# Gates computed first, the chunk inverse handed out in portions, and later stand-offs in a two-block layer kernel

## The chip, the cores and the metric

The kernel runs on one core of a Trainium2 chip. The metric is the device time of one execution in microseconds; lower is better. The time before is the median of three runs.

## The reference

The input is one sequence of 256 positions by 1024 channels in float32. Two layer blocks follow one another. The first has a short convolution branch and a gated delta rule branch, both from one wide projection `w_in`; their gated sum goes through `w_o`, and a convolution feed-forward follows. The second has dilated attention and retention, and a feed-forward. The change is mainly in the gated delta rule (8 heads, chunks of 64, key and value width 128):

```python
beta = jax.nn.sigmoid(b)
g = -jnp.exp(A_log) * jax.nn.softplus(a + dt_bias)
...
G = jnp.cumsum(g, axis=-1)
decay = jnp.exp(jnp.where(tril, G[..., :, None] - G[..., None, :], -jnp.inf))
L = jnp.where(strict, jnp.einsum('bnhid,bnhjd->bnhij', k_beta, k) * decay, 0.0)
rhs = jnp.concatenate([v_beta, k_beta * jnp.exp(G)[..., None]], axis=-1)
sol = lax.linalg.triangular_solve(eye + L, rhs, left_side=True, lower=True)
...
o = o * lax.rsqrt(jnp.mean(o * o, axis=-1, keepdims=True) + EPS) * norm_g
o = o * jax.nn.silu(z)
```

The projections a and b give the gates, q, k, v go through a causal convolution of four taps and a silu, and q and k are normalised by head. The kernel solves the triangular system by chunks of 128 with the inverse of (I + L).

## The kernel before

**Jobs and units.** Nearly all the time goes into dense products of 256 tokens with weights that are read once. A *job* is one block of weights of 1 MB (128 rows by 2048 values), and it has two halves, the *units*. SyncE (SP) loads a job into one of three raw buffers (`load_w`, line 316). For each unit ScalarE (ACT) copies 128x1024 values to a rounded high part H (`split_act`, line 143), and VectorE (DVE) subtracts it from the raw values to give the low part L (`tt`, line 146). TensorE (PE) then runs 24 matmuls of 128x256 in three passes of eight: Hh·H, Hl·H and Hh·L (`dense`, line 334). There are three buffers for H and L, and the split runs two units ahead of the matmuls.

**The order of the work.** Every engine works through its own queue in order. The program text makes that order: a main loop over the units advances *generators*. One kind evacuates a finished job (convolution taps, sigmoids, splits of the result), the other kind (`auxes`) carries the gated delta rule, the norms and the attention. Each `yield` hands control back, so the number of yields sets how many units later the next instructions stand in each queue. An instruction that waits holds everything behind it on its engine. The constants at the top of the file (`SUB_W`, `GAM_Y`, `AT_Y`, `SC_Y`, `SC_Z` and others) are such counts of yields; `D1_Q` and `SC_Q` choose which engine issues every second of some transfers.

**Order of the jobs.** K (4 jobs), ab (the gates, one small job of one unit), Q (4), the three parts of the short convolution interleaved (12), V (4), `w_a_out`, ga, z, gb, `w_b_out`, `w_o`, then the up and down jobs and the second block.

**The gated delta rule, by lines.** `gates` (from line 429) turns the projected a and b to tokens-by-heads with two small matmuls (line 432), takes sigmoid and exponentials on ACT, and evaluates a polynomial for the softplus by 28 small operations of 128x16 on GpSimd (POOL), ending in the tile `gg`. `gdn_decay` sums `gg` along the chunk with PE (lines 486 and 488), sends the sums through memory to all partitions (lines 498, 499) as `gam`, waits until the keys are done, and applies sixteen exponentials of 128x128, each with its own bias. `gdn_keys` transposes K (line 537) and sums squares on ACT. `gdn_main` forms K·Kᵀ (line 561), multiplies by `gam` on DVE and by beta on POOL into `U`, and scatters 32x32 blocks of U to memory with four transfers (line 573). They come back as `ebd`, 64 partitions of 32x32 (line 576).

**The substitution.** `subst` inverts the 64 blocks in place. `step(eng, i)` for i = 31 down to 1 is a multiply into `bt` and a subtraction from `ebd`, i·(32−i) values a partition, each depending on the one before. All 31 steps are issued to POOL at once. Then POOL clears Dm and Em, DVE copies the inverse transposed (line 596), two transfers write both forms to memory (line 598), and eight gathers bring the blocks to Dm and Em, 128x2048 each (line 604). `gdn_main` goes on when `sub_ok` is set: K·Qᵀ has been formed before (line 629), and now the first matmuls with Dm (line 649) and the doubling of the inverse follow (lines 651 to 672). Later the output o is normalised: rsqrt of q's norm and of o's norm, each twelve or so small operations on POOL, a multiply of o, and PE's transposes of o (line 772), which feed the `w_b_out` jobs.

**Elsewhere.** `up_evac` in the feed-forward multiplies gate and value on POOL (line 146) and splits the product, first high on ACT (`mh`), then low on DVE (`ml`). In the attention `qk_evac` scales q and k on ACT, and takes squares head by head (`jk`); an rsqrt on POOL (48 columns) follows, and PE transposes q and k (line 1167) `AT_Y` yields later.

## Time and profile before

| What | us |
|---|---|
| Median of three runs | 1133.23 (1131.77 to 1134.21) |
| Profiled execution | 1132.61 |
| Its span, first to last instruction | 1130.7 |
| PE busy | 1102.9 (98%) |
| DVE busy | 738.9 (65%) |
| ACT busy | 587.5 (52%) |
| POOL busy | 247.4 (22%) |
| Mean granted TensorE clock | 0.991 |

The span is what the trace covers, and the profiled execution has 1.9 us more around it. In the rows, a name like `L` or `ebd` is a tile of the program, with buffer numbers left out; line 146 is a helper that stands for all additions and multiplications, so tiles tell more than lines. An entry in brackets at a row's end is the time for which the engine stood idle before it, and the instruction that ended the wait.

### The profile page before, as it was taken

To read this page: it belongs to the slowest core of one execution; us is meant where nothing else is said; L and a number is where in the kernel's file an instruction comes from. 1 tells how busy PE (TensorE), PEld (TensorE's weight loads), DVE (VectorE), ACT (ScalarE), POOL (GpSimd) and SP (SyncE) were. 2 spreads that over 40 slices of the span, in tenths; PEclk is the share of its full clock that TensorE was granted. 3 is DMA by queue.
4 is the path that set the end of the run, shared out by engine and by line. 5 is a ranking of instruction groups with operands and counts; after the bars stand their busy time and mean duration, and the time that the engine had idled before them with its cause. 6 is when DMAs were issued, how large, how long until landed. Compare 5 with 4: busy or idle time off the path is not lost.

```text
span 1130.7 us, 20224 instructions
## 1 busy us (share of the span) xinstructions
PE 1102.9 (98%) x8340; PEld 1048.8 (93%) x8340; DVE 738.9 (65%) x985; ACT 587.5 (52%) x958; POOL 247.4 (22%) x290
## 2 busy tenths in 40 slices
PE   9989969999899999999999999999999999999998
PEld 8989969999899999999878799889999999898997
DVE  5767766345577888778854467557686657655554
ACT  7866425376445444444687544555474445444442
POOL 3575976021401222222201300001340001000000
PEclk9989989999999999999999999999999999999999
DMA  7566537343465466555565444453536555555652
GB/s 246 168 203 182 156 95 203 113 138 124 150 199 175 150 209 201 187 188 185 200 247 174 162 150 150 145 190 113 174 127 222 187 187 177 175 193 190 193 191 75
DMA packets 156080, 194.83 MB, mean 172 GB/s; under 512 B 6702, under 2 KB 133029, under 8 KB 155732
## 3 DMA queue, kind: packets, MB, share of 16 engines
q1 hardware_dynamic: 153888, 191.57, 52.1%
q0 software_dynamic: 848, 1.30, 0.5%
q8 instruction: 65, 1.06, 0.4%
q10 hardware_dynamic: 1252, 0.67, 0.2%
q14 instruction: 27, 0.22, 0.1%
HBM read 191.68 MB, written 1.84 MB: 171 GB/s over the span
## 4 chain that ended last, share of the span: by engine, by line
PE 75%; issue 8%; POOL 8%; DVE 5%; ACT 3%; DMA 1%; POOLq 0%; ACTq 0%; DVEq 0%
PE d L334 55%; PE x L334 13%; POOL bt L146 2%; POOL ebd L146 2%; DVE L L146 2%; ACT H L143 1%; DVE w L149 1%; POOL w L146 1%; DVE nl L149 1%; ACT w L143 1%; POOL nw L146 1%; PE x L1192 0%; ACT jk L143 0%; DVE X L146 0%; PE x L1167 0%
## 5 line engine op out<-in xcount | busy, mean ns | idle before, releaser
L146 DVE TENSOR_TENSOR L<-raw,H 128x1024 fp32r<-128x1024 f32 x354 | 443.5, 1259 | 252.0 <-ACT H L143 247.6
L143 ACT ACTIVATE H<-raw 128x1024 fp32r<-128x1024 f32 x355 | 369.7, 1053 | 192.6 <-PE d L334 134.0
L334 PE MATMUL d<-Hh,L 128*128 128x256 f32 x576 | 79.8, 282 | 9.3 <-DVE L L146 9.3
L334 PE MATMUL d<-nh,H 128*128 128x256 f32 x608 | 83.6, 279 | 2.2 <-ACT H L143 1.4
L334 PE MATMUL d<-Hh,H 128*128 128x256 f32 x576 | 84.6, 290 | 0.1
L334 PE MATMUL d<-nh,L 128*128 128x256 f32 x608 | 82.0, 277 | 0.0
L334 PE MATMUL d<-nl,H 128*128 128x256 f32 x608 | 81.9, 277 | 0.0
L334 PEld LDWEIGHTS d<-Hh,L 128*128 128x128 f32 x576 | 73.1, 192 | 9.5 <-DVE L L146 9.5
L334 PEld LDWEIGHTS d<-nh,H 128*128 128x128 f32 x608 | 76.7, 188 | 4.2 <-ACT H L143 1.6
L334 PE MATMUL d<-Hl,H 128*128 128x256 f32 x576 | 79.5, 281 | 0.0
L334 PEld LDWEIGHTS d<-Hh,H 128*128 128x128 f32 x576 | 74.3, 194 | 1.1 <-issue 0.4
L334 PEld LDWEIGHTS d<-nl,H 128*128 128x128 f32 x608 | 75.2, 188 | 0.0
L334 PEld LDWEIGHTS d<-nh,L 128*128 128x128 f32 x608 | 75.1, 188 | 0.0
L334 PEld LDWEIGHTS d<-Hl,H 128*128 128x128 f32 x576 | 73.1, 192 | 0.1
L334 PE MATMUL d<-H,x2h 128*128 128x512 f32 x208 | 57.3, 397 | 1.1 <-ACT H L143 1.1
L334 PE MATMUL d<-L,x2h 128*128 128x512 f32 x208 | 56.2, 392 | 0.0
L334 PE MATMUL d<-H,x2l 128*128 128x512 f32 x208 | 56.0, 391 | 0.0
L334 PE MATMUL d<-x2h,H 128*128 128x256 f32 x384 | 54.3, 284 | 0.0
L334 PE MATMUL d<-x2h,L 128*128 128x256 f32 x384 | 52.2, 278 | 0.0
L334 PE MATMUL d<-x2l,H 128*128 128x256 f32 x384 | 52.1, 278 | 0.0
L334 PEld LDWEIGHTS d<-x2h,H 128*128 128x128 f32 x384 | 48.7, 189 | 0.7
L146 POOL TENSOR_TENSOR gr<-w,w 128x512 f32<-128x512 f32 x8 | 11.8, 1472 | 171.4 <-ACT w L143 171.4
(394 smaller groups left out, 1939.7 us busy)
## 6 DMA issues: line engine op xcount, KB each, us to landing
raw<-in_w_in_dram SPq DMA_DIRECT2D x86, 1024.0 KB, 5.1
raw<-in_w_up_dram SPq DMA_DIRECT2D x38, 1024.0 KB, 5.3
raw<-in_w_down_dram SPq DMA_DIRECT2D x27, 1024.0 KB, 4.9
raw<-in_w_proj_b_dram SPq DMA_DIRECT2D x8, 1024.0 KB, 5.1
raw<-in_w_a_out_dram SPq DMA_DIRECT2D x4, 1024.0 KB, 6.4
raw<-in_w_b_out_dram SPq DMA_DIRECT2D x4, 1024.0 KB, 5.2
raw<-in_w_o_dram SPq DMA_DIRECT2D x4, 1024.0 KB, 5.2
raw<-in_w_out_dram SPq DMA_DIRECT2D x4, 1024.0 KB, 5.5
```

Of the source, the lines that this page charges most:

```text
L143: ACT.activation(out=out, in_=in_, func=func, **kw)
L146: eng.tensor_tensor(out=out, in0=a, in1=b, op=op)
L149: DVE.scalar_tensor_tensor(out=out, in0=in0, scalar=scalar, in1=in1, op0=op0, op1=op1)
L334: PE.matmul(out, lhsT=x if swap else w, rhs=w if swap else x, start=first and ps == 0, stop=last and ps == group[-1] and group is (order o ...
```

## The change

The ab job moves to the front of the list, and `id2`, which its transposes need, is made at the start. The polynomial of the gates moves from POOL to DVE, in four portions between yields. `gam` no longer waits for the keys; POOL subtracts the sums (four additions of 128x512), and two exponentials of 128x1024 take the place of the sixteen. The norm of k follows them. A yield in the key loop goes away, so that K·Kᵀ and what follows come earlier. All four scatters are issued by POOL. In the substitution the first eight steps go to DVE and the rest stays on POOL, with a yield after every four or two steps. The transposed copy moves to POOL, the clearing of Em, Dm and P stands between the transfers, and Em is gathered first. The rsqrt of q moves to DVE, right after Q·Kᵀ, with its square kept as `rq2`; the transposes of o come one unit later. V's sigmoid waits two yields longer, Q's one longer, K's as long as before (`SG_Y`). The first gate-times-value unit has a yield more, `AT_Y` is 5, one yield in the attention evacuation moves, and `late` splits a unit into two passes of two k-blocks each for two jobs.

```diff
-SUB_W = 11
+SUB_W = 1
-AT_Y = 4
+AT_Y = 5
-GAM_Y = 2
+GAM_Y = 4
-D1_Q = 0
+D1_Q = 2
+SG_Y = {8: 3, 0: 4, 16: 5}
-SC_Y = 3
-SC_Q = 1
-SC_Z = 3
+SC_Y = 2
+SC_Z = 4
...
             h3, l3 = w3(H, kh, n), w3(L, kh, n)
...
+            for ks in ((0, 1), (2, 3)) if late and half == 1 else (range(kh),):
...
-            yield
-            yield
-            yield
+            for _ in range(SG_Y[base]):
+                yield
             act(a2, acc, AF.Sigmoid)
...
-        tt(POOL, fl(s), fl(s), fl(u), MUL)
-        tt(POOL, fl(s2), fl(s), fl(s), MUL)
-        pts(fl(p), fl(s2), 1.0 / 17, MUL, 1.0 / 15, ADD)
+        tt(DVE, fl(s), fl(s), fl(u), MUL)
+        tt(DVE, fl(s2), fl(s), fl(s), MUL)
+        ts(fl(p), fl(s2), 1.0 / 17, MUL, 1.0 / 15, ADD)
+        yield
         for k in range(6, -1, -1):
-            tt(POOL, fl(p), fl(p), fl(s2), MUL)
-            pts(fl(p), fl(p), 1.0 / (2 * k + 1), ADD)
+            tt(DVE, fl(p), fl(p), fl(s2), MUL)
+            ts(fl(p), fl(p), 1.0 / (2 * k + 1), ADD)
+            if k in (2, 4):
+                yield
...
-        while "k_ok" not in gd:
-            yield
-        gdn_norm_k()
...
             tt(DVE, gam[:, sl, :], gam[:, sl, :], negm.unsqueeze(1).to_broadcast([128, 4, 128]), ADD)
-            if q % 2 == 0 and EXP1:
-                continue
-            yield
-            for u in range(8 * (q // 2) if EXP1 else 4 * q, 4 * q + 4):
-                act(gam[:, u, :], gam[:, u, :], AF.Exp, bias=ng[:, u:u + 1])
+            tt(POOL, gam[:, sl, :], gam[:, sl, :], ng[:, sl].unsqueeze(2).to_broadcast([128, 4, 128]), ADD)
+            if q % 2:
+                yield
+        for q in range(2):
+            yield
+            sl = slice(8 * q, 8 * q + 8)
+            act(gam[:, sl, :], gam[:, sl, :], AF.Exp)
         act(eg.rearrange("p a b -> p (a b)"), ng, AF.Exp, scale=-1.0)
+        while "k_ok" not in gd:
+            yield
+        gdn_norm_k()
...
             for i in range(31, 0, -1):
-                step(POOL, i)
+                step(POOL if i < 24 else DVE, i)
+                if i % (2 if 7 < i < 24 else 4) == 0:
+                    yield
...
-            POOL.memset(gd["Dm"], 0.0)
-            POOL.memset(gd["Em"], 0.0)
-            DVE.tensor_copy(out=blk, in_=eb.rearrange("p r c -> p c r"))
-            for dd, sb in ((d3, blk), (d2, eb)):
-                POOL.dma_start(out=dd.rearrange("b u r c -> (b u) r c"), in_=sb)
+            POOL.dma_start(out=d2.rearrange("b u r c -> (b u) r c"), in_=eb)
+            POOL.tensor_copy(out=blk, in_=eb.rearrange("p r c -> p c r"))
+            POOL.dma_start(out=d3.rearrange("b u r c -> (b u) r c"), in_=blk)
+            POOL.memset(gd["Em"], 0.0)
+            yield
             POOL.memset(gd["Dm"], 0.0)
...
-            for dd, dst in ((d3, gd["Dm"]), (d2, gd["Em"])):
+            for dd, dst in ((d2, gd["Em"]), (d3, gd["Dm"])):
...
+        yield
+        ts(sq, sq, EPS, ADD)
+        rsqrt(rq, sq, 16, dve=True)
+        rq2 = cst("rq2", [128, 16])
...
-        ts(sq, sq, EPS, ADD)
-        rsqrt(rq, sq, 16)
...
+    jobs.append(Job(load_w("w_in", 0, 8, 7168, 128), ab_mm, ab_evac, halves=1, start=(gates,), split=ab_split))
     for p in range(4):
         fm_job("w_in", 4096 + 256 * p, "x", qkv_evac(K, 8, p), start=(gdn_keys,) if p == 3 else ())
-    jobs.append(Job(load_w("w_in", 0, 8, 7168, 128), ab_mm, ab_evac, halves=1, start=(gates,), split=ab_split))
...
                 tt(POOL, md, ff.pop(("gs", m)), acc, MUL)
                 yield
+                if m == 0:
+                    yield
...
-            yield
             for i in range(2):
+                yield
                 for h in range(4):
```

Three places show how the queues change. The first is the polynomial of the gates (`spp`, `ss`; `KQ` is K's result, `w` a convolution's working tile). Before, on POOL:

```order
L146 TENSOR_TENSOR KQ_118<-w_541,w_542 128x256
L146 TENSOR_TENSOR w_674<-w_674,w_675 128x2x255
L146 TENSOR_TENSOR ss__657<-ss__657,su 128x16
L146 TENSOR_TENSOR ss_658<-ss__657 128x16
L168 TENSOR_SCALAR spp<-ss_658 128x16
L146 TENSOR_TENSOR spp<-spp,ss_658 128x16
L166 TENSOR_SCALAR spp<-spp 128x16
```

After, on DVE, `L` being a weight split:

```order
L146 TENSOR_TENSOR L_400<-raw_195,H_399 128x1024
L146 TENSOR_TENSOR ss__341<-ss__341,su 128x16
L146 TENSOR_TENSOR ss_342<-ss__341 128x16
L155 TENSOR_SCALAR spp<-ss_342 128x16
L146 TENSOR_TENSOR L_440<-raw_246,H_439 128x1024
L149 SCALAR_TENSOR_TENSOR w_433<-d_365,prm,w_433 128x254 x2
L149 SCALAR_TENSOR_TENSOR w_433<-d_365,prm,w_433 128x253 x2
L146 TENSOR_TENSOR spp<-spp,ss_342 128x16
L153 TENSOR_SCALAR spp<-spp 128x16
```

The polynomial has left POOL's queue and stands between DVE's splits, a portion at a time. The second place is the substitution's start and the copy on DVE. Before:

```order
L146 TENSOR_TENSOR w_2017<-d_1962,keep_1951 128x512
L146 TENSOR_TENSOR L_2020<-raw_1862,H_2019 128x1024
L146 TENSOR_TENSOR yal_1233<-w_2017,yah_1232 128x512
L596 COPY ebd_1391<-ebd_1391 64x1024
L146 TENSOR_TENSOR L_2058<-raw_1862,H_2057 128x1024
L146 TENSOR_TENSOR L_2094<-raw_1923,H_2093 128x1024
```

After:

```order
L146 TENSOR_TENSOR ebd_1290<-ebd_1290,bt_1490 64x28x4
L146 TENSOR_TENSOR L_1494<-raw_1210,H_1493 128x1024
L146 TENSOR_TENSOR AT_1475<-x_1476,gam_741 128x512
L146 TENSOR_TENSOR bt_1529<-ebd_1290 64x135
L146 TENSOR_TENSOR ebd_1290<-ebd_1290,bt_1529 64x27x5
L146 TENSOR_TENSOR bt_1532<-ebd_1290 64x156
```

Before, DVE had no step and had the copy of `ebd` ahead of a split; after, it has eight steps in two portions with a split between, and no copy. The third place is the end of the substitution on POOL (`scr` is memory). Before:

```order
L146 TENSOR_TENSOR bt_1674<-ebd_1391 64x31
L146 TENSOR_TENSOR ebd_1391<-ebd_1391,bt_1674 64x31
L594 MEMSET Dm_2051 128x2048
L595 MEMSET Em_2050 128x2048
L598 DMA scr_1386<-ebd_1391 64x1024
L598 DMA scr_1385<-ebd_1391 64x1024
L146 TENSOR_TENSOR w_2087<-w_2087,w_2088 128x2x255
L604 DMA Dm_2051<-scr_1386 32x16x32 x2
L604 DMA Em_2050<-scr_1385 32x16x32 x2
```

After:

```order
L146 TENSOR_TENSOR bt_1951<-ebd_1290 64x31
L146 TENSOR_TENSOR ebd_1290<-ebd_1290,bt_1951 64x31
L600 DMA scr_1284<-ebd_1290 64x1024
L601 COPY ebd_1290<-ebd_1290 64x1024
L602 DMA scr_1285<-ebd_1290 64x1024
L603 MEMSET Em_1992 128x2048
L605 MEMSET Dm_1993 128x2048
L608 MEMSET P_2062 128x2048
L614 DMA Em_1992<-scr_1284 32x16x32 x2
L614 DMA Dm_1993<-scr_1285 32x16x32 x2
L146 TENSOR_TENSOR w_2094<-w_2094,w_2095 128x2x255
```

The copy has come to POOL between the two transfers, a third memset has come ahead of the gathers, and the addition of V's convolution (`w`) now stands behind them. On PE the first matmuls with Dm stand behind the same unit as before, V's last.

## Rows read from the trace of the kernel before

**Rows 1.** Page, busy time by engine: busy us, share of the span, instructions.

```profile
PE 1102.9 (98%) x8340; PEld 1048.8 (93%) x8340; DVE 738.9 (65%) x985; ACT 587.5 (52%) x958; POOL 247.4 (22%) x290
```

**Rows 2.** What PE waited for: us in total, times, longest.

```profile
PE d L334 <- DVE L L146: 9.3, 1, 9.3
PE x L486 <- POOL gg L146: 3.5, 1, 3.5
PE x L772 <- POOL o L146: 3.4, 2, 3.2
PE x L1167 <- POOL k L146: 2.7, 2, 1.7
PE d L334 <- ACT H L143: 2.5, 2, 1.4
...
PE x L909 <- DVE sr L149: 0.3, 1, 0.3
```

**Rows 3.** Windows: us, busy of each engine, then PEclk (granted clock), DMA share, GB/s.

```profile
64.10:70.10 6.00, 6.00 (x27) 5.57 (x28) 0.21 (x1) 2.93 (x10) 5.26 (x7) 0.50 0.07 24
163.00:169.00 6.00, 2.37 (x11) 2.38 (x12) 6.00 (x7) 0.26 (x1) 2.81 (x3) 0.50 0.31 71
292.40:295.60 3.20, 3.20 (x15) 3.20 (x16) 1.58 (x2) 0.63 (x1) 3.20 (x6) 0.50 0.69 245
```

**Rows 4.** PE timeline (start, us, engine, line, operation, out<-in, [idle before]); long wait, Dm.

```profile
166.63 2.07 PE L334 MATMUL d<-Hh,L 128*128 128x256 f32 x8 [9.28 <-DVE L L146]
168.50 1.54 PE L334 MATMUL d<-Hh,H 128*128 128x256 f32 x8
169.88 1.07 PE L334 MATMUL d<-Hl,H 128*128 128x256 f32 x8
...
179.85 1.89 PE L649 MATMUL x<-Dm,U 128*128 128x64 f32 x16
```

**Rows 5.** Timeline of POOL: the last products of the gates.

```profile
63.84 0.36 POOL L146 TENSOR_TENSOR gg<-spp,nA 128x8 f32<-128x8 f32 x2
```

**Rows 6.** Timeline of DVE: a small operation and a weight split.

```profile
364.79 0.16 DVE L149 SCALAR_TENSOR_TENSOR sr<-nw,sr 128x2 f32<-128x2 f32 x1
364.87 1.23 DVE L146 TENSOR_TENSOR L<-raw,H 128x1024 fp32r<-128x1024 f32 x1
```

**Rows 7.** Timeline of ACT: a table load and what follows it.

```profile
26.97 1.28 ACT L143 ACT_TABLE_LOAD   x1
28.26 0.63 ACT L143 ACTIVATE w<-w 128x512 f32<-128x512 f32 x1
```

**Rows 8.** Timeline of POOL: U's last product and the scatters' issue (two, one by one).

```profile
101.22 1.04 POOL L146 TENSOR_TENSOR U<-U,bk 128x512 f32<-128x512 f32 x1 [1.76 <-DVE dec L568]
102.56 1.40 POOL L573 DMA_DIRECT2D scr<-U  x2 [0.30 <-POOL U L146]
```

**Rows 9.** DMA issues, 95 to 182 us: KB each, median us from issue to landing.

```profile
ebd<-scr POOLq DMA_DIRECT2D x1, 256.0 KB, 3.8
...
scr<-U POOLq DMA_DIRECT2D x2, 64.0 KB, 4.2
```

**Rows 10.** Timeline of POOL: the substitution and the first memset.

```profile
111.78 0.25 POOL L146 TENSOR_TENSOR bt<-ebd 64x31 f32<-64x31 f32 x1 [2.19 <-DMA ebd<-scr]
...
122.37 0.59 POOL L146 TENSOR_TENSOR bt<-ebd 64x207 f32<-64x207 f32 x1
...
123.70 0.59 POOL L146 TENSOR_TENSOR bt<-ebd 64x220 f32<-64x220 f32 x1
124.37 1.69 POOL L146 TENSOR_TENSOR ebd<-ebd,bt 64x220 f32<-64x220 f32 x1
...
161.12 1.81 POOL L594 MEMSET Dm<- 128x2048 f32 x1
```

**Rows 11.** Timeline of DVE: the copy.

```profile
161.17 4.27 DVE L596 COPY ebd<-ebd 64x1024 f32<-64x1024 f32 x1 [9.47 <-POOL ebd L146]
```

**Rows 12.** Line 604, the gathers of Dm and Em: issue to landing.

```profile
DMA to landing us min/median/max: 6.0/6.1/8.4
```

More of the change, by code (lines that the diff above doesn't have):

```diff
@@ L274, in startup @@
         param_cols(0, 128)
+        gd["id2"] = cst("id2", [32, 16])
+        tt(POOL, gd["id2"], ident[0:32, 0:16], ident[0:32, 16:32], ADD)
         for ft2 in range(4):
@@ L294, in startup_rest @@
         tt(POOL, gg, prm[:, 1, 96:104], prm[:, 1, 104:112], MUL)
-        gd["id2"] = cst("id2", [32, 16])
-        tt(POOL, gd["id2"], ident[0:32, 0:16], ident[0:32, 16:32], ADD)
         for ft2 in range(4):
@@ L335, in dense, with fm_job @@
                               stop=last and ps == group[-1] and group is (order or ORDER)[-1], skip_group_check=True)
-    def fm_job(name, c0, src, evac, k0=0, kt=8, n=256, ps_box=None, last=True, **kw):
+    def fm_job(name, c0, src, evac, k0=0, kt=8, n=256, ps_box=None, last=True, late=False, **kw):
         nf = n // 128
@@ L350, in mm @@
             xh, xl = S[src]
-            dense([(box[j // 2][:, j % 2, :], h3[:, k, 128 * j:128 * j + 128], l3[:, k, 128 * j:128 * j + 128],
-                    xh[:, half * kh + k, :], xl[:, half * kh + k, :], False,
-                    fresh and k == 0 and j % 2 == 0, last and half * kh + k == kt - 1 and j % 2 == 1)
-                   for k in range(kh) for j in range(nf)])
+            for ks in ((0, 1), (2, 3)) if late and half == 1 else (range(kh),):
+                dense([(box[j // 2][:, j % 2, :], h3[:, k, 128 * j:128 * j + 128], l3[:, k, 128 * j:128 * j + 128],
+                        xh[:, half * kh + k, :], xl[:, half * kh + k, :], False,
+                        fresh and k == 0 and j % 2 == 0, last and half * kh + k == kt - 1 and j % 2 == 1)
+                       for k in ks for j in range(nf)])
         jobs.append(Job(load_w(name, k0, kt, c0, n), mm, (lambda: evac(box)) if evac else None, **kw))
@@ L448, in gates @@
         fl = lambda t: t.rearrange("p a b -> p (a b)")
[L449 to L451 removed]
+        tt(DVE, fl(s), fl(s), fl(u), MUL)
+        tt(DVE, fl(s2), fl(s), fl(s), MUL)
+        ts(fl(p), fl(s2), 1.0 / 17, MUL, 1.0 / 15, ADD)
+        yield
         for k in range(6, -1, -1):
[L453 to L457 removed]
+            tt(DVE, fl(p), fl(p), fl(s2), MUL)
+            ts(fl(p), fl(p), 1.0 / (2 * k + 1), ADD)
+            if k in (2, 4):
+                yield
+        ts(fl(s), fl(s), -2.0, MUL)
+        tt(DVE, fl(p), fl(p), fl(s), MUL)
+        tt(DVE, fl(p), fl(p), fl(m), SUB)
         for c in range(2):
[L459 removed]
+            tt(DVE, g[:, c, :], p[:, c, :], nA[:, 0, :], MUL)
         yield
@@ L593, in subst @@
             gd["Em"], gd["Dm"] = alloc([16, 128], what="Em"), alloc([16, 128], what="Dm")
+            POOL.dma_start(out=d2.rearrange("b u r c -> (b u) r c"), in_=eb)
[3 more added lines that the diff above has]
+            yield
             POOL.memset(gd["Dm"], 0.0)
-            POOL.memset(gd["Em"], 0.0)
-            DVE.tensor_copy(out=blk, in_=eb.rearrange("p r c -> p c r"))
-            for dd, sb in ((d3, blk), (d2, eb)):
-                POOL.dma_start(out=dd.rearrange("b u r c -> (b u) r c"), in_=sb)
+            yield
+            gd["P"] = alloc([16, 128], what="P")
+            POOL.memset(gd["P"], 0.0)
             for _ in range(SC_Y):
                 yield
-            for dd, dst in ((d3, gd["Dm"]), (d2, gd["Em"])):
+            for dd, dst in ((d2, gd["Em"]), (d3, gd["Dm"])):
                 for b in range(4):
                     bs = slice(32 * b, 32 * b + 32)
-                    (POOL, (ACT, SP, POOL)[SC_Q])[b % 2].dma_start(out=dst[bs, :, bs], in_=dd[b].rearrange("u r c -> r u c"))
+                    (POOL, SP)[b % 2].dma_start(out=dst[bs, :, bs], in_=dd[b].rearrange("u r c -> r u c"))
             free(ebd)
@@ L633, in gdn_main @@
         free(gam, KQ[0])
+        yield
+        ts(sq, sq, EPS, ADD)
+        rsqrt(rq, sq, 16, dve=True)
+        rq2 = cst("rq2", [128, 16])
+        ts(rqs, rq, 128 ** -0.5, MUL)
+        tt(DVE, rq2, rqs, rqs, MUL)
         while "sub_ok" not in gd:
             yield
-        Em, Dm = gd["Em"], gd["Dm"]
-        P = alloc([16, 128], what="P")
-        POOL.memset(P, 0.0)
+        Em, Dm, P = gd["Em"], gd["Dm"], gd["P"]
         def half32(t, h):
@@ L746, in gdn_main @@
         fo = cst("fo", [128, 16])
-        ts(sq, sq, EPS, ADD)
-        rsqrt(rq, sq, 16)
-        POOL.tensor_scalar(out=rqs, in0=rq, scalar1=128 ** -0.5, scalar2=None, op0=MUL)
         yield
-        tt(POOL, sof, sof, rqs, MUL)
-        tt(POOL, sof, sof, rqs, MUL)
+        tt(POOL, sof, sof, rq2, MUL)
         POOL.tensor_scalar(out=sof, in0=sof, scalar1=1.0 / 128, scalar2=EPS, op0=MUL, op1=ADD)
@@ L1093, in _build @@
         for gate in (True, False):
-            fm_job("w_up", (0 if gate else 2816) + 256 * m, "xf", up_evac(m, gate), delay=(DG if gate else DV) if m == 0 else 0)
+            fm_job("w_up", (0 if gate else 2816) + 256 * m, "xf", up_evac(m, gate), delay=(DG if gate else DV) if m == 0 else 0,
+                   late=m == 0 and gate)
         if 0 < m < 9:
@@ L1117, in go @@
                 act(dst[:, i, :], box[i], AF.Copy, scale=S["r12"][:, i:i + 1])
-            yield
             for i in range(2):
+                yield
                 for h in range(4):
@@ L1551, in _build @@
     for m in range(16):
-        fm_job("w_up_2", 256 * m, "xn", up2_evac(m))
+        fm_job("w_up_2", 256 * m, "xn", up2_evac(m), late=m == 0)
         if m > 0:
```

4 lines of the change are left out of this document (removed).

## The prediction

> **What bounds the kernel now.** I read the page's busy times first: TensorE (PE) is busy 1102.9 us, 98% of the span [rows 1]. So the time is the matmuls plus the moments when PE stands still or runs slowly, and nothing else can be gained by this change, which leaves the number of matmuls as it is. The second view is what PE waited for [rows 2]: 9.3 us for a VectorE (DVE) weight split, 3.5 for the gates on GpSimd (POOL), 3.4 at the transposes of o, 2.7 at the attention transposes, 2.5 for a ScalarE (ACT) copy, 0.3 at a norm sum. With smaller ones it is under 25 us. The third view is the granted clock in windows behind these waits [rows 3]: 0.50 from 64.1 to 70.1, from 163 to 169 and from 292.4 to 295.6, that is 1.2 instead of 2.4 GHz, each right after a wait of over 3 us; work done there costs half its length again. That is 3.0 to 3.2 us after the gates, 1.6 after the transposes, and 1.45 after the long wait, where PE was only there from 166.6: its two first passes of eight matmuls took 2.07 and 1.54 instead of 1.07 [rows 4]. Shorter waits in the list were not followed by such a stretch.
>
> The profiled execution took 1132.6 us, 1.9 over its span and 0.6 under the median of the runs; I sum against it and add 0.6 at the end. Some 0.2%, 2.3 us, is what a measurement of this kernel can tell from no change.
>
> **The change, part by part**
>
> **Gates first.** Before, the polynomial stands on POOL behind K's convolution adds; its last product ends at 64.2 [rows 5], and PE waits. After, the ab job runs first, and 28 small operations stand on DVE in four portions between weight splits. A DVE operation of this size takes 0.16 us [rows 6]; with spacing I take 0.2, so 5.6 us of DVE work in four portions of about 1.4, which the lead of the splits over PE covers. Counted along DVE's queue gg is there at about 43.6 us, PE comes at about 45.3. Gone: 3.5 us of wait and 3.2 of half clock. Added: K's first unit now needs the second weight load, about 0.5 us later at the start, and two table loads stand on ACT ahead of the copy for the fifth unit. The load took 1.28 us and the next activation began 0.01 us after it ended [rows 7]; two of them, less what ACT was ahead, and the later DVE split: 1.0. Together −6.7 + 1.5 = **−5.2**; if the start costs nothing −6.7, if both loads come through whole −3.6.
>
> The Trainium skill, "ScalarE: Activation LUTs", section "What ACT_TABLE_LOAD costs", gives each switch about 1.28 us plus a drain of 1.38, 2.66 in all. By that the two loads would take 2.8 us more and this part would be −2.4; the trace shows no such drain between load and activation, so the row decides.
>
> **Decay.** Two wide exponentials replace sixteen; POOL gets four additions more, each about the length of the 1.04 us multiply of U [rows 8], plain work in a queue that has room there. But K's and Q's sigmoids on ACT now wait for adds behind them: 0 to 1 us for the copies of two units; I take **+0.5**.
>
> **Substitution, start.** K·Kᵀ stands three units (8.3 us) earlier on PE, and all before it is 5 us earlier; the chain through the norm of k on POOL, one unit later, eats part. Counted along POOL, U's last product is done at about 94.3 instead of 102.3. All four scatters are issued by POOL, two more than before at 0.7 [rows 8]; they land 4.2 us after issue, the load of the blocks 3.8 [rows 9]. So the first step, at 111.8 before [rows 10], comes at about 104.8. Eight steps go to DVE in two portions, 1.9 and 2.65 us, with a split between: done at about 111 (estimated as 0.16 us an instruction and the split's rate of 1.23 us for 1024 elements [rows 6]). By the two queues the splits behind them keep 2 to 4 us in hand; **+0.5** (0 to 2).
>
> **Substitution, rest.** 23 steps on POOL began at 122.4 and ended at 161.1 [rows 10]: 38.7 us. In it a subtraction took 1.69 us with a DVE split beside it, while the multiply of the same shape just before took 0.59; with the unheld length for every shape the 46 instructions come to 30.5, so holds make up 8.2 us. All fell in the 29.3 us before 151.7, since DVE then stood still waiting for POOL [rows 11]. In the changed kernel DVE goes on, so the last 9.4 us stretch at the same rate, 8.2 on 21.1: +3.6. End: 111 + 38.7 + 3.6 = 153.3.
>
> **The copy moves from DVE to POOL.** This ends the wait: DVE stood 9.47 us for the last step and copied for 4.27 [rows 11], with all splits behind it. Gone: 9.28 us and 1.45 of half clock, **−10.7**.
>
> **What is late next.** The inverse needs Dm at the same place of PE's queue as before, behind V's last unit. From the last step to Dm: the scatter's issue 0.6, the copy on POOL about 2.9 (1024 elements a row at the rate of the step of 220 elements in 0.59; at worst DVE's 4.27), a second issue 0.6, three memsets of 1.81 [rows 10], three gathers issued at 0.67, and 6.1 from issue to landing, at worst 8.4 [rows 12]. Sum 17.6, at worst 20.6. So Dm lands at about 170.9. PE got there at 179.85 [rows 4]; less 17.5 for the two waits and their slow clock, plus 2.5 for the costs above, it now arrives at 164.9. **A new wait of 6.0 us**, and half clock behind it, 1.45 to 3.2 by the other places, 2.0: **+8.0**. V's sigmoid on ACT stands behind a POOL add that comes after the gathers' issue, and falls into the same moment.
>
> **Transposes of o.** The rsqrt of q, on POOL just before them, moves to DVE long before, and the transposes go one unit later. 3.4 of wait and 1.6 of half clock go, the rsqrt of the output's norm still ends just when PE arrives: 0.3 stays. **−4.7.**
>
> **One yield in the first gate-times-value unit** puts ACT's copy of the product, which waits for a POOL multiply, behind the next weight copy: of the 2.5 us in the list [rows 2] the 1.4 here go, **−1.2**. The other 1.1, behind eight squarings, stays; the moved yield in the attention evacuation only swaps neighbours. **Splitting a unit in two passes** (late) cures 0.4 in the second block; in the first the norm sum ends last anyway [rows 2]. **−0.4.** **Attention transposes two units later**: 2.7 go, **−2.5**.
>
> Sum: −5.2 + 0.5 + 0.5 − 10.7 + 8.0 − 4.7 − 1.2 − 0.4 − 2.5 = −15.7, so 1116.9, and 1117.5 on the scale of the median.
>
> **The rivals**
>
> *No new wait.* Without any hold the 23 steps would take about 30.5 us (38.7 less 8.2). If they end by 147.3, Dm is in time: 8.0 less, **1109.5**. For it: where DVE stood still, from 151.7 on, the steps ran without a hold; against it: DVE is given its splits, and eight steps, at just that time. 0.2.
>
> *The wait at its worst.* Slow copy, slow landing, end at 154: Dm at 174.6, a wait of 9.7 with 3.2 of clock, **1122.4**. 0.16.
>
> *The scatters are late.* POOL's issues are held by DVE work as its adds are: the hold is 1.1 us [rows 10], four make 4.4; and if these four land as slowly as the slowest gather (8.4 for 4.2 [rows 9, 12]) it is 8.6 later in all. The first step then holds DVE until 113, PE waits for splits, and all up to Dm is 8.6 late: **1126.1**. Against it: both issues in the trace took 0.7 with DVE at work beside them [rows 8]. 0.07.
>
> The Trainium skill, "SBUF — State Buffer", section "A bandwidth-pool intuition that's wrong (but worth ruling out)", has this as a trap for transfers issued by GpSimd: about 620 ns alone, about 3100 beside a VectorE copy. By that four issues would be 9.6 us late, and the time 1127.1; the trace bears out the first figure and shows no case of the second.
>
> *Slower: POOL held nearly always.* Place: the 46 instructions of the 23 steps. A hold costs 1.1 [rows 10]; before, 7 or 8 fell on the first 28. Each further one moves the end, Dm and PE by its length. From 17 more (27 of 46, the end at 171.3) the change is slower by over 2.3 us; at 20 more it is 22 us, **1139.5**. Against it: it takes over twice the share of held instructions that the trace shows. 0.04.
>
> *The gates don't lead on DVE.* If the portions queue behind late splits, PE waits at the decay matmuls as before, up to 6.7: **1124.2**. 0.05.
>
> **How the numbers follow.** My forecast has 0.48, and its 1117.5 is the predicted time. The old waits go in every case and the new one's size is what is open, so the first three cases are faster whole. Late scatters and late gates (0.12 together) are faster singly; where both go wrong, and draw splits and sigmoids with them, the gain is used up: of their 0.12 I give 0.04 to the same and 0.02 to slower. With the 0.04 of the held POOL that is 0.90, 0.04, 0.06. The range holds the forecast, no new wait with a start that costs nothing (1109.5 − 1.5 = 1108) and the late scatters (1126), with 1 us more below for the terms taken at +0.5.
>
> **What would show it.** Right: no wait at the decay matmuls; no DVE wait of 9 us; a new PE wait of 4 to 9 us at the first Dm matmul with a 0.50 window behind it; no wait at the transposes of o over 0.5; 1.1 us left for ACT's copy. Wrong, if the Dm wait is missing or over 12, if splits wait behind the DVE steps near 107 us, or if a wait at the start exceeds 2 us.

## The result, and the profile after

The changed kernel takes **1151.8 us** (1151.0 to 1152.4, four runs) where the kernel before takes 1132.5 in the same session (1130.9 to 1134.2): a ratio of 1.016 (1.014 to 1.018), 19 us slower. The forecast was 1117.5 with a range of 1107 to 1126, so it is wrong in sign and 34 us off. The profiled execution took 1151.0, its span is 1149.2.

The page's busy times of the changed kernel, in us, with the share of the span and the number of instructions:

```profile
PE 1127.2 (98%) x8340; PEld 1073.6 (93%) x8340; DVE 750.5 (65%) x1033; ACT 586.0 (51%) x944; POOL 241.7 (21%) x245
```

Beside [rows 1] one thing stands out: PE executes the same 8340 matmuls and is busy 24.3 us longer. What it stood idle has become less. Its list of waits (line, what it waited for, us in total, times, the longest):

```profile
PE x L663 <- DMA Dm<-scr: 7.9, 1, 7.9
PE d L334 <- DVE L L146: 6.2, 6, 2.4
PE d L334 <- ACT H L143: 1.7, 2, 1.0
PE d L271 <- DVE warm L210: 1.4, 1, 1.4
PE x L920 <- DVE sr L149: 0.7, 1, 0.7
```

Against [rows 2] the waits for the gates, for the long weight split, at the transposes of o and at the attention transposes are gone; the new wait for Dm is there; and the weight splits are late six times by a little. The sum falls from 24 to 18 us. A reader who stops at the waits would call the change a success.

Two windows show where the 18.5 us of span come from: from the start to the first matmul with Dm (L663), and from there to the end. The columns are the stretch, its length, then the busy time and number of instructions of PE, the weight loads, DVE, ACT and POOL, and last the granted clock, the share of the DMA engines and GB/s. First the kernel before:

```profile
0.00:179.80 179.80, 165.43 (x1352) 162.62 (x1353) 126.09 (x173) 109.98 (x227) 118.36 (x163) 0.96 0.59 181
179.80:1130.00 950.20, 937.43 (x6990) 886.15 (x6989) 612.86 (x813) 477.55 (x731) 129.04 (x128) 1.00 0.52 171
```

The same of the changed kernel:

```profile
0.00:187.40 187.40, 170.99 (x1353) 165.53 (x1353) 137.90 (x224) 107.89 (x217) 115.35 (x132) 0.97 0.58 178
187.40:1149.00 961.60, 956.22 (x6988) 908.10 (x6988) 612.65 (x810) 478.15 (x729) 126.33 (x113) 0.99 0.51 168
```

Dm is reached 7.6 us later, after the same matmuls. Behind it PE is idle for 5.4 instead of 12.8 us, as forecast, yet busy 18.8 us longer with the same matmuls at nearly the same granted clock; the other 5.6 of the 24.3 us lie ahead of Dm. So there are two losses: matmuls that are slower each, and an early part that arrives later instead of earlier.

The slower matmuls can be seen in PE's timeline, in the middle of an undisturbed stretch (start, length, engine, line, out<-in, shapes, matmuls in the row). Before:

```profile
405.28 1.07 PE L334 MATMUL d<-nh,L 128*128 128x256 f32 x8
406.18 1.07 PE L334 MATMUL d<-nh,H 128*128 128x256 f32 x8
407.09 1.07 PE L334 MATMUL d<-nl,H 128*128 128x256 f32 x8
```

And the changed kernel in the same kind of unit:

```profile
420.78 1.12 PE L334 MATMUL d<-nh,H 128*128 128x256 f32 x8
421.74 1.12 PE L334 MATMUL d<-nl,H 128*128 128x256 f32 x8
422.70 1.12 PE L334 MATMUL d<-nh,L 128*128 128x256 f32 x8
```

Eight matmuls follow one another at 0.905 us before and at 0.96 us after, 113 and 120 ns for one. Nothing waits. Over the whole program, most passes of eight keep 113 or 118 ns a matmul before (about 370 and 410 passes), and 120 after (about 680).

### The profile page after: what moved, and what is told of

Same layout as the page of the kernel before. It is cut to its first block, busy times and chain, and to the rows that moved or that the text cites. A ratio compares the mean times of both kernels' runs of the same rounds, so it can differ in the third digit from the quotient of the medians.

```text
span 1149.2 us, 20224 instructions
## 1 busy us (share of the span) xinstructions
PE 1127.2 (98%) x8340; PEld 1073.6 (93%) x8340; DVE 750.5 (65%) x1033; ACT 586.0 (51%) x944; POOL 241.7 (21%) x245
## 4 chain that ended last, share of the span: by engine, by line
PE 84%; POOL 5%; DVE 4%; ACT 3%; DMA 2%; issue 2%; POOLq 0%; DVEq 0%; ACTq 0%
PE d L334 63%; PE x L334 13%; POOL bt L146 2%; POOL ebd L146 2%; DVE L L146 2%; ACT jk L143 1%; ACT H L143 1%; DVE w L149 1%; DMA Dm<-scr 1%; POOL gam L146 1%; PE x L663 0%; PE x L1181 0%; PE x L1206 0%; DMA scr<-U 0%; DMA xtm<-in_x_dram 0%
## 5 line engine op out<-in xcount | busy, mean ns | idle before, releaser
L143 ACT ACTIVATE H<-raw 128x1024 fp32r<-128x1024 f32 (+1 forms) x355 | 369.9, 1053 | 205.2 <-PE d L334 152.4
L334 PE MATMUL d<-Hh,L 128*128 128x256 f32 x576 | 82.2, 286 | 6.2 <-DVE L L146 6.2
L334 PE MATMUL d<-nh,H 128*128 128x256 f32 x608 | 85.9, 283 | 0.0
L334 PE MATMUL d<-nl,H 128*128 128x256 f32 x608 | 85.7, 283 | 0.0
L334 PE MATMUL d<-nh,L 128*128 128x256 f32 x608 | 85.7, 283 | 0.0
L334 PEld LDWEIGHTS d<-nh,H 128*128 128x128 f32 x608 | 79.2, 191 | 1.2
L334 PEld LDWEIGHTS d<-nh,L 128*128 128x128 f32 x608 | 78.6, 192 | 0.0
L334 PEld LDWEIGHTS d<-nl,H 128*128 128x128 f32 x608 | 78.5, 192 | 0.0
L334 PEld LDWEIGHTS d<-x2h,L 128*128 128x128 f32 x384 | 49.5, 191 | 0.0
```

What stands on the lines that cost most here:

```text
L143: ACT.activation(out=out, in_=in_, func=func, **kw)
L334: PE.matmul(out, lhsT=x if swap else w, rhs=w if swap else x, start=first and ps == 0, stop=last and ps == group[-1] and group is (order o ...
```

## The experiments

### Is it the place of the tiles?

The changed kernel keeps one constant more, `rq2`: 16 floats, 64 B in each partition. It lies ahead of the large tiles that are made after the constants, so they all move by 64 B. In the built programs the streamed activations (`Hh`, `nh` and the like) begin at 64 modulo 256 before, and at 128 after. The raw weights and their parts H and L lie ahead of the constants (the pools `raw` and `hl` are opened first) and stay at 128 in both kernels, so of the two operands in SBUF of these matmuls only the streamed one has moved. Theory A: this place sets the pace of the matmuls. Theory B: something that the change does (its traffic, its order) makes them longer. A pad behind the constants moves everything and computes nothing:

```diff
         rq2 = cst("rq2", [128, 16])
+        cst("pd2", [128, 16])
```

> The changed kernel with an unused constant of 64 bytes a partition behind rq2. The new constant rq2 (64 bytes) had moved every large tile behind the constants, so that the activations that the 256-column matmuls stream start at 0 modulo 128 bytes instead of 64; this puts them back to 64. Theory A (the tiles' place sets the matmul pace): passes of eight return from 120 ns a matmul to 113 to 118, PE's busy time falls by about 24 us, and the time is 1151.8 - 24 = 1128 (1124 to 1131). Theory B (the new order of the queues sets the pace): the pace stays at 120 and the time at 1150 to 1153.

For the cleanest test the same line went into the kernel before, which is then given the place, and nothing else, of the changed one.

> The kernel before with the same unused 64 bytes at the same place, and no other change; its streamed tiles now start at 0 modulo 128 bytes. Theory A: 120 ns in nearly all 256-column passes, PE busy 24 us more, 1132.5 + 24 = 1156 (1151 to 1160). Theory B: 1131 to 1134, passes of 113 and 118 as before.

Two more pads, of 8 and of 24 floats, took the places between.

> The changed kernel with 32 unused bytes: streamed tiles at 32 modulo 128. Theory A says only that the pace depends on the place: if what counts is 0 against not 0, as at 64 (1124 to 1131); if it is the distance, between the two (1130 to 1150). Theory B: 1150 to 1153.

> The changed kernel with 96 unused bytes: streamed tiles at 96 modulo 128. Theory A: as at 32 if the distance from the stationary tiles (0 modulo 128) counts in both directions, 1124 to 1150. Theory B: 1150 to 1153.

And 48 floats (192 B) put every tile that PE streams in the changed kernel back to the place modulo 256 that it has in the kernel before.

> The changed kernel with 192 unused bytes behind rq2: every large tile starts where it started in the kernel before modulo 256 bytes (streamed activations at 64). Theory A2 (the place modulo 256 decides: at 64 a pace of 113 is to be had, at 192 hardly, at 0 and 128 it is 120): passes of 113 in the feed-forwards again, PE busy near 1103, time 1151.8 - 24 = 1128 (1122 to 1132), so the change without its accident of place is worth 4 us (0 to 10). Rival C (only the distance modulo 128 counts, and the rest is the new order of the queues): as with 64 bytes, 1139 to 1143.

What was measured (the ratio is to the kernel before in the same session; busy time and pace of a matmul of 256 columns from the profiles). The kernel before took 1132.5 us in the first session, 1132.3 in that of the four pads, 1135.7 in that of the 192 B, and 1132.4 and 1133.2 in two later ones, so times of different sessions are to be compared by their ratios:

| kernel | streamed tiles begin at, mod 256 | time, us | ratio | PE busy | pace, ns |
|---|---|---|---|---|---|
| before | 64 | 1132.5 | 1 | 1102.9 | 113, 118 |
| after | 128 | 1151.8 | 1.016 (1.014 to 1.018) | 1127.2 | 120 |
| before, 64 B | 128 | 1152.3 | 1.017 (1.013 to 1.021) | 1127.2 | 120 |
| after, 32 B | 160 | 1141.4 | 1.008 (1.006 to 1.010) | 1115.2 | 116 to 117 |
| after, 64 B | 192 | 1141.9 | 1.008 (1.005 to 1.011) | 1115.4 | 118, few 113 |
| after, 96 B | 224 | 1156.8 | 1.021 (1.017 to 1.025) | 1133.6 | 118 to 121 |
| after, 192 B | 64 | 1133.7 | 0.999 (0.997 to 1.001) | 1103.4 | 113, 118 |

The row that decides is the kernel before with 64 B of an unused constant. Its busy times and one of its lines (x count | busy us, mean ns | idle before):

```profile
PE 1127.2 (98%) x8340; PEld 1074.5 (93%) x8340; DVE 739.4 (64%) x985; ACT 589.7 (51%) x958; POOL 246.5 (21%) x290
L334 PE MATMUL d<-nh,L 128*128 128x256 f32 x608 | 85.3, 283 | 0.0
```

DVE, ACT and POOL have the instruction counts of the kernel before, while PE is busy as long as in the changed kernel to the tenth. And the changed kernel with 192 B:

```profile
PE 1103.4 (98%) x8340; PEld 1047.6 (93%) x8340; DVE 751.7 (66%) x1033; ACT 584.0 (52%) x944; POOL 241.5 (21%) x245
L334 PE MATMUL d<-nh,L 128*128 128x256 f32 x608 | 82.5, 278 | 0.0
```

There the counts are those of the changed kernel and PE's time is that of the one before. B falls: the place alone makes and takes away the whole 24 us of PE. A holds for direction and size at 128 and at 64; its simple form, in which a step of 64 B that leaves a multiple of 128 restores the pace, does not, since 64 B more gave back only half. Nor is it the distance from a multiple of 128: with 32 B and with 96 B the tiles stand equally far from one, yet the first took 1141.4 us and the second, expected at 1124 to 1150, 1156.8, the slowest of all. With 192 B PE's time came back as A2 had it, but the gain of 4 us did not: by the ratio it is 1.5, within the noise.

The form A2, that the place modulo 256 counts, held there. Taken tile by tile it would say that each tile's own place decides for that tile. The tiles `mh` and `ml` stand at 192 in the kernel before and run at 118; 128 B ahead of the pools of working tiles bring them to 64, and shift `w` and `bt`, which PE does not stream in these passes, by as much.

```diff
+    tmp("pd3", (32,), bufs=1)
```

> As the run with 192 bytes, with 128 unused bytes ahead of the pool of mh and ml, whose start goes from 192 to 64 modulo 256. Theory A2 (192 gives 118, 64 can give 113): the passes that stream mh and ml fall from 118 to 113 in the first feed-forward, 66 passes of eight at 4.6 ns, 2.4 us less; all other passes stay as they were. If the place does not decide for single tiles, mh stays at 118 and the time the same within 1 us.

It took 1133.6 us, 1.0005 (0.9987 to 1.0022): the passes with `mh` stayed at 118, and those with `nh`, which had not moved, went from a mix to nearly all 118 (PE busy 1109.3). The finer form falls, since `mh` at 64 kept its 118. At 64 the pace is 113 in some passes and 118 in others, and which it is differs between the profiled executions of kernels whose PE instructions and addresses are alike; that stays open below.

### What the change is worth at the old place

With the place put back, the changed kernel takes as long as the one before. Yet the waits at the gates, at the long DVE split and at both transposes are gone in it too. Its windows:

```profile
0.00:185.80 185.80, 164.62 (x1352) 158.80 (x1353) 139.16 (x224) 107.66 (x216) 115.17 (x132) 0.98 0.58 179
185.80:1130.00 944.20, 938.82 (x6988) 888.83 (x6988) 612.50 (x811) 476.34 (x729) 126.33 (x113) 1.00 0.52 171
```

Behind Dm it is 6.2 us shorter than the kernel before (944.7 to the end of its span, against 950.9), and Dm itself is 6.0 later. So the early part costs what the late part gains. I took the later edits alone (rsqrt of q on DVE, the transposes of o, `late`, the yields, `AT_Y`) into the kernel before, with the constant and a pad that keeps the place:

```diff
-AT_Y = 4
+AT_Y = 5
...
+        ts(sq, sq, EPS, ADD)
+        rsqrt(rq, sq, 16, dve=True)
+        rq2 = cst("rq2", [128, 16])
+        cst("pd2", [128, 48])
...
+            fm_job("w_up", (0 if gate else 2816) + 256 * m, "xf", up_evac(m, gate), delay=(DG if gate else DV) if m == 0 else 0,
+                   late=m == 0 and gate)
```

> The kernel before with only the later parts of the change: rsqrt of q early on VectorE, the transposes of o a unit later, the yield in the first gate-times-value unit, late, AT_Y 5, the moved yield; 192 unused bytes behind rq2, so that no large tile moves modulo 256. Gates, substitution and copy stay as they were. Theory P (the part up to Dm gained nothing, the part behind it did what was forecast): 8.8 us less than before by the terms of the forecast, 6.4 by the stretch behind Dm in the run with 192 bytes; ratio 0.992 to 0.995. Rival (the pace drifts elsewhere and takes it): 0.998 to 1.002.

It took **1124.7 us, 0.9931 (0.9915 to 0.9947)**: faster than both kernels. Its windows beside the two above:

```profile
0.00:181.40 181.40, 165.08 (x1352) 162.00 (x1353) 132.16 (x187) 109.88 (x227) 119.42 (x163) 0.96 0.60 180
181.40:1125.00 943.60, 938.39 (x6990) 888.44 (x6988) 611.12 (x810) 478.10 (x731) 125.36 (x113) 1.00 0.52 172
```

The stretch behind Dm has the same gain, and Dm comes 4.4 us earlier than with the whole change (1.6 later than before; this profiled execution took 1127.6). The waits for the gates and for the split, 4.7 and 9.7 here, on which the forecast took off most, still stand in this kernel, and it is faster than the one without them.

### The chain that the early part hangs on

The chain that ended last of the changed kernel between 95 and 190 us tells why (start, length, engine, tile, line):

```profile
by line: POOL bt L146 22.8%; POOL ebd L146 22.3%; issue 10.1%; DMA Dm<-scr 7.7%; DMA scr<-U 5.4%; DMA ebd<-scr 4.1%; DVE L L146 3.3%; PE x L663 2.9%; DVE keep L149 2.7%; DVE bt L146 2.3%; POOL ebd L601 2.2%; DVE ebd L146 2.2%; POOL scr L577
...
103.22 1.04 POOL U L146
104.55 2.02 POOL scr L577 x3
106.57 5.17 DMA scr<-U
112.27 3.89 DMA ebd<-scr
...
167.75 1.12 POOL ebd L146
169.73 2.13 POOL ebd L601
...
179.90 7.36 DMA Dm<-scr
187.40 2.79 PE x L663 x12
```

From U to Dm, PE's matmuls are not in it at all: the last product of U, the scatters, the load of the blocks, 31 steps with one DVE weight split between them, the copy, the clearing and the gathers. Whatever PE gains in that time by waiting less, it gives back at Dm. Five points of this chain in six kernels, in us from the span's start:

| kernel | last K·Kᵀ matmul | U's last product ends | first step | last step ends | first matmul with Dm |
|---|---|---|---|---|---|
| before | 99.1 | 102.3 | 111.8 | 161.1 | 179.9 |
| later edits alone | 100.0 | 102.9 | 112.3 | 162.0 | 181.4 |
| after | 93.3 | 104.3 | 116.2 | 168.9 | 187.4 |
| after, 192 B | 91.7 | 102.7 | 114.7 | 167.4 | 185.8 |
| later edits, copy on POOL | 98.9 | 102.0 | 112.7 | 165.9 | 180.2 |
| later edits, gates first | 103.7 | 109.0 | 119.2 | 169.0 | 188.2 |

*K·Kᵀ comes 7.4 us earlier, U does not.* POOL's timeline of the kernel with 192 B (in brackets what it waited before, and for whom):

```profile
85.74 0.21 POOL L146 TENSOR_TENSOR nw<-grr 128x16 f32<-128x16 f32 x1 [1.46 <-DVE grr L172]
96.36 2.95 POOL L146 TENSOR_TENSOR U<-U,bk 128x512 f32<-128x512 f32 x2 [1.75 <-DVE U L146]
101.67 1.04 POOL L146 TENSOR_TENSOR U<-U,bk 128x512 f32<-128x512 f32 x1 [2.36 <-DVE dec L572]
103.01 2.67 POOL L577 DMA_DIRECT2D scr<-U  x4 [0.29 <-POOL U L146]
110.50 0.57 POOL L580 DMA_DIRECT2D ebd<-scr  x1 [4.83 <-DMA scr<-U]
```

POOL multiplies what DVE has multiplied first, and DVE's four products of U stand in DVE's queue between weight splits and the short convolution's work for later units (`keep`, `yal`); POOL waits for them twice. The last of the four starts at nearly the same time in the kernel before and in the kernel with 192 B:

```profile
100.47 0.68 DVE L146 TENSOR_TENSOR U<-x,gam 128x512 f32<-128x512 f32 x1
100.91 0.68 DVE L146 TENSOR_TENSOR U<-x,gam 128x512 f32<-128x512 f32 x1
```

In the second of them DVE worked without a pause from 88.1 to 105.0. The first step then comes 12.0 us after U instead of 9.5, for four scatters on POOL's queue instead of two (2.67 us of issue).

*The 23 steps on POOL hold longer.* They take 45.9 us here (121.4 to 167.4) and 38.7 in the kernel before [rows 10].

Five kernels tried the points of this chain one by one, all with the 192 B. First Dm's place in PE's order, three units later (`SC_Z` 4 to 7):

> As the run with 192 bytes, and SC_Z 7 in place of 4: the matmuls with Dm stand three units (8.3 us) later in PE's queue. If the wait at Dm (7.9 us and 1.6 of half clock behind it in the changed kernel) is a real loss, it goes and the time is 7 to 9.5 less than with 192 bytes alone. If the work behind is then late instead (the transposes of o, w_b_out), 0 to 4 less.

1132.5 us, 0.9986 (0.9967 to 1.0004): no gain. The wait for Dm is gone and two others have its size:

```profile
PE d L334 <- ACT H L143: 8.7, 4, 6.0
PE d L334 <- ACT Oh L143: 3.5, 2, 2.4
```

PE's timeline puts the 6.0 where the wait for Dm was, and ACT's says why: V's sigmoid waited 10.7 us for a POOL addition that stands behind the gathers, and the weight copies stand behind the sigmoid.

```profile
184.98 2.07 PE L334 MATMUL d<-yah,H 128*128 128x256 f32 x8 [6.01 <-ACT H L143]
181.89 0.63 ACT L143 ACTIVATE w<-w 128x512 f32<-128x512 f32 x1 [10.67 <-POOL w L146]
```

So the same POOL queue reaches PE by a second way. Then all steps on POOL again (the copy stays there):

```diff
-                step(POOL if i < 24 else DVE, i)
+                step(POOL, i)
```

> As the run with 192 bytes, but all 31 steps of the substitution on POOL, the yields as in the change. Theory P (all up to Dm hangs on the substitution, so what DVE's first steps save counts whole): the first eight steps take 10.6 us instead of 6.7, so +4 (+2 to +6). Rival (DVE's backlog from waiting for the blocks is what costs): -2 to 0.

1136.7 us, 1.0017 (1.0000 to 1.0034): 3 us longer than with the eight steps on DVE, as Theory P had it. The first eight steps took 10.6 us instead of 6.7 and the rest 43.8 instead of 45.9. The wait for Dm of 16.4 instead of 9.8 is not all theirs: in this profiled execution U already ended 2.5 us later, and PE came to Dm 2.9 sooner. Two scatters back on ACT (`D1_Q` 2 to 0):

> As the run with 192 bytes, with every second scatter of U on ScalarE's queue as before (D1_Q 0). Theory P: the blocks are back some 2 us sooner (from the first issue to the blocks 9.4 us before, 11.6 in the changed kernel), Dm too, and the time is 1.5 to 2.5 less. If the chain up to Dm does not decide, or ScalarE is held by the issue: -0.5 to +2.

1135.6 us, 1.001 (0.9993 to 1.0027), so the expected gain did not come in the total. The load of the blocks was issued 3.5 us sooner (106.98 for 110.50), but the first step, on DVE, began 0.4 later (115.13 for 114.70) and Dm came only 0.8 sooner. ACT's queue tells why:

```profile
103.62 1.06 ACT L143 ACTIVATE H<-raw 128x1024 fp32r<-128x1024 f32 x1 [4.45 <-issue]
```

ACT held its weight copies until U was done and the two scatters were issued, so DVE's splits ahead of the first step were late. PE waited 2.5 us at 102 for such a copy and came to Dm at 179.3 instead of 176.0, so the wait for Dm fell to 5.7 without Dm being much earlier. That is the rival's case, an ACT held by the issue. PE also ran more passes at 118 (busy 1110.9 against 1103.4) although its instructions are the same. Then a shorter tail, with Dm gathered before Em, P cleared after the gathers, and one yield more behind the last step, so that V's first addition on POOL stands ahead of the gathers:

```diff
-SUB_W = 1
+SUB_W = 2
-SC_Z = 4
+SC_Z = 6
...
-            gd["P"] = alloc([16, 128], what="P")
-            POOL.memset(gd["P"], 0.0)
...
-            for dd, dst in ((d2, gd["Em"]), (d3, gd["Dm"])):
+            for dd, dst in ((d3, gd["Dm"]), (d2, gd["Em"])):
...
+            gd["P"] = alloc([16, 128], what="P")
+            POOL.memset(gd["P"], 0.0)
```

> As the run with 192 bytes, with the tail of the substitution shortened and made room for: Dm gathered ahead of Em, P cleared later, the gathers behind V's first addition on POOL (SUB_W 2), Dm three units later on PE (SC_Z 6). Theory P (the wait at Dm and the sigmoid behind POOL's tail are both of that chain): the 9.8 us at Dm and the 1.6 of half clock go, 3.5 come back at the o transposes as in the run with SC_Z 7; 7 to 9 less than with 192 bytes. Rival (something else on the way is as late): 0 to 2 less.

> As the last, with Dm two units later (SC_Z 5). Theory P: about 2 us of wait at Dm stay, under 1 at the o transposes; 7 to 10 less than with 192 bytes. Rival: 0 to 2 less.

1130.6 (0.9983, 0.9966 to 1.0000) and, with `SC_Z` 5, 1128.3 us (0.9967, 0.9947 to 0.9986). Both remove the wait for Dm, both leave 3.1 us behind V's sigmoid and 2.7 to 3.5 for the split of o (`Oh`, near 312 us). By the ratios they gain 0.5 and 2.3 us on the kernel with 192 B (0.9987) instead of 7 or more; 0 to 2 was the rival's figure. Neither is as fast as the later edits alone.

### The early edits one at a time

On top of the later edits, the copy on POOL instead of DVE:

```diff
-            DVE.tensor_copy(out=blk, in_=eb.rearrange("p r c -> p c r"))
+            POOL.tensor_copy(out=blk, in_=eb.rearrange("p r c -> p c r"))
```

> The kernel before with the later parts (1124.7) and the copy of the inverse on GpSimd instead of VectorE, nothing else. Theory P (Dm's landing decides when PE goes on, and it landed just when PE came, so VectorE's 9.7 us hole only hid behind it): the wait at the weight split goes, a wait of the same size or 1 to 5 us more stands at Dm, since the copy is now in POOL's own chain and the last steps are held by the splits; time +1 to +5. The forecast's step (-10.7 for the hole, +8.0 for the new wait): -3.

1128.3 us, 0.9951 (0.9935 to 0.9968): by the ratios 2.3 us slower than without, though the two intervals overlap. The forecast's own step had 3 us of gain here. The DVE wait of 9.7 is gone, and PE waits 10.0 for ACT:

```profile
PE d L334 <- ACT H L143: 10.9, 2, 10.0
174.01 0.63 ACT L143 ACTIVATE w<-w 128x512 f32<-128x512 f32 x1 [12.66 <-POOL w L146]
```

It is V's sigmoid again, not Dm as expected. With eight steps on DVE besides:

> As the run before, with the first eight steps on VectorE in two portions and yields as in the change. Theory P: the steps take 6.7 us instead of 10.6, so Dm comes 4 us sooner than with the copy alone, 3 to 5 us less than that run, and within 2.5 of the later parts alone.

1127.8 us, 0.9952 (0.9938 to 0.9966): nothing more, against an expected 3 to 5. The first step began at 114.7 instead of 112.7, and the last ended at 166.2, as without them (165.9). And the later edits with the gates first, but without the copy or the steps:

> The kernel before with the later parts and the gates first, their polynomial in four portions on VectorE; substitution and copy as before. Forecast's step: -5.2. Theory Q (VectorE's portions delay splits: waits of 0.9 and 2.5 us at 40 and 47 and half clock behind, 5 in all, and K times K transposed comes a unit later): 7.9 go, 5 come, -3 to +1.

1129.1 us, 0.9969 (0.9953 to 0.9985), 4 us slower than with the gates at their old place. The wait for the gates is gone as hoped; in its place U comes 6 us later and the wait for the split grows from 9.7 to 12.6:

```profile
PE d L334 <- DVE L L146: 16.0, 3, 12.6
```

Both expectations for it missed. Here the decay, unlike in the changed kernel, still came by sixteen exponentials, so this run prices the gates' new place in the old surroundings only.

## Why the prediction was wrong

The error of 34 us has three parts that add up to it: 18.7 from the place (spans of 1149.2 without and 1130.5 with the 192 B); 14.9 from the way to Dm, which at the old place came 5.9 later than before and not, as forecast, 8.9 earlier (170.9 for 179.85); and 0.6 from all behind it, which gained 6.2 for 6.8.

**First failed step: "nothing else can be gained by this change, which leaves the number of matmuls as it is".** The number stayed and their length did not. I took the time of a matmul as given because neither its shape nor its operands changed, and never asked what `rq2` moves. It costs 64 B, and 24.3 us of PE; how that place acts on a matmul is not shown. The kernel's list of constants even holds a tensor `pad` of 32 B that nothing reads (`LINE_PAD`), a reason to ask what stands behind it.

**Second failed step: "Counted along POOL, U's last product is done at about 94.3".** It ended at 102.7 at the old place (104.3 in the changed kernel). K·Kᵀ did move by 7.4 us; but I followed POOL's queue and left out that each of U's products is first made on DVE, where the last of them began at 100.91 for 100.47 before. With 1.5 more for scatters and load, the first step was at 114.7 instead of 104.8.

**Third, a term of the wrong size: "+3.6" for the longer holds.** The 23 steps took 45.9 us, 7.2 more than before. With DVE no longer standing still the holds grew about twice as much as I took.

These two add up: the last step ended at 167.4 instead of 153.3. From there the forecast's tail of 17.6 us was near, 18.4, in part by luck: the copy took 2.1 for 2.9, and from the last gather's issue to Dm's landing it was 7.4 (in the changed kernel) for 6.1. Dm landed at 185.8 instead of 170.9.

**Fourth, the sum of the early part.** I took PE's waits off one by one (−5.2, −10.7) and set one new wait against them. But from U to Dm PE's progress is decided by a chain on other engines, so a wait taken off ahead of Dm comes back at Dm unless that chain gets shorter. It got longer. PE's own arrival was wrong too. I had it at Dm at 164.9, and at the old place it came at 176.0, for most of it because DVE's splits and one ACT copy were late seven times on the way, by 9.8 us together, where I had put 2.5 in all. So the size of the new wait, 7.9 (9.8 at the old place) for a forecast of 6.0, is luck: it began 11 us later than forecast at the old place and ended 15 us later.

**Right:** no wait at the decay matmuls; no 9 us of DVE standing still; a wait for Dm between 4 and 9 with a window of half clock behind it; no wait over 0.5 at the transposes of o; 1.0 us left for ACT's copy. For the later part the forecast had −8.8; measured alone it is −7.7.

**Smaller misses.** The gates' 28 small operations were taken at 0.2 us, 5.6 in all. The trace of the kernel before has 22 of them on POOL; on DVE these 22 took 7.5 us, and `gg` was there at 47.9 instead of 43.6. DVE's timeline of the changed kernel shows equal operations at both prices:

```profile
44.19 0.16 DVE L146 TENSOR_TENSOR spp<-spp,ss 128x16 f32<-128x16 f32 x1
44.39 1.27 DVE L153 TENSOR_SCALAR spp<-spp 128x16 f32<-128x16 f32 x1
46.40 0.74 DVE L146 TENSOR_TENSOR spp<-spp,smx 128x16 f32<-128x16 f32 x1
47.17 0.71 DVE L146 TENSOR_TENSOR gg<-spp,nA 128x8 f32<-128x8 f32 x2
```

POOL was at work on 128x510 and 128x256 values beside the slow ones; that it held them is argued from the times alone. The split behind these portions came late, and PE waited 2.3 us at 49. And I wrote that waits under 3 us were not followed by half clock: in the changed kernel waits of 2.27 and 2.40 us were, as PE's timeline and the windows behind them show (column PEclk, after POOL's):

```profile
49.08 1.22 PE L334 MATMUL d<-Hh,L 128*128 128x256 f32 x8 [2.27 <-DVE L L146]
138.86 1.89 PE L334 MATMUL d<-Hh,L 128*128 128x256 f32 x8 [2.40 <-DVE L L146]
```

```profile
51.00:54.00 3.00, 3.00 (x15) 2.74 (x14) 2.90 (x4) 1.91 (x4) 2.19 (x1) 0.54 0.91 307
138.90:141.90 3.00, 3.00 (x15) 3.00 (x16) 3.00 (x4) 0.00 (x0) 2.69 (x5) 0.53 0.00 0
```

But with the 192 B a wait of 2.48 us that ended at 49.3 was not, so the length of a wait does not settle it (first row below). And [rows 3] leaves out a fourth stretch of half clock in the kernel before, which no wait preceded: PE had run narrow matmuls of the inverse, of 64 and 32 columns, without a pause (second row).

```profile
49.40:52.40 3.00, 3.00 (x25) 2.77 (x26) 3.00 (x6) 1.77 (x5) 0.34 (x1) 1.00 0.65 185
193.40:196.40 3.00, 3.00 (x15) 3.00 (x15) 1.07 (x3) 0.00 (x0) 0.00 (x0) 0.50 0.02 5
```

The rival on the other side, POOL held nearly always, had a last step at 171.3 as its sign; it came at 168.9, but by a late start for the larger part, and the 19 us of the result are not its doing.

**What stays open.** What makes a pass run at 113 or at 118 ns at one and the same place. Executions of the later edits alone took from 1122.3 to 1127.6 us at the same granted clock of 0.992; only one of them has a trace, so that they differ in this pace is not shown. How the place acts: the weights' own places did not change, so it is not theirs that matters, but every tile behind the constants moved at once, and `mh` moved to 64 kept 118 while `nh`, which stayed at 64, ran at 118 too in that execution; that the streamed tile's own place decides is only argued. Why U came 6 us later with the gates first in the old surroundings, beyond that K·Kᵀ itself was 3.7 us later and POOL waited for DVE's products. And the wide exponentials and the earlier K·Kᵀ were never run by themselves.

## What to carry to other kernels

Where PE is busy 98% of the time, look at what a change does to the addresses of the operands before counting waits: compare the pace of an undisturbed pass, and try the old kernel with an unused constant of the same size. And before taking a wait off the sum, find the chain that sets the next meeting point (here Dm): only what shortens that chain counts, and each hand-over between engines in it has to be followed in the queue of both. Edits are best timed in groups, since here one group gained 7.7 us and the other lost some 6.

## What the hardware showed that I had not expected

- The start of the tiles behind the constants in SBUF, the streamed ones among them, changes the pace of the same matmul while the weights' tiles stay at 128: 113 or 118 ns at 64 modulo 256, 118 at 192, 116 to 117 at 160, 120 at 128, 118 to 121 at 224. Over 8340 matmuls that is up to 30.7 us of PE (1102.9 to 1133.6).
- At 64 the pace is not settled by PE's instructions and addresses: two kernels in which these are the same had PE busy 1103.4 and 1110.9 us, in one profiled execution each.
- Waits of 2.3 and 2.4 us, not only those over 3, were followed by a granted clock of about 0.5, that is 1.2 GHz, while one of 2.48 us was followed by 1.00; and after narrow matmuls without any wait it was 0.50 too (193.4 to 196.4 us in the kernel before).
- DVE operations on 16 elements a row, mostly 0.16 to 0.18 us, took up to 1.27 us beside POOL's additions.
